# A chunked scan in which ScalarE makes one mask term before its other copies of a step, and VectorE adds the other mask term at the start of the next step

## The chip, the cores and the metric

The kernel runs on one core of one Trainium2 chip. The metric is the device time of one execution in microseconds (us), the median of three runs. Engines are named as in the profile: PE (TensorE matmul), PEld (its weight load), DVE (VectorE), ACT (ScalarE), POOL (GpSimd), SP (SyncE).

## The reference, cut to what matters

Two hybrid attention layers are followed by two layers whose token mixer is a bidirectional Mamba-2 scan beside windowed attention. The change lies in the scan, which runs once in each of the last two layers:

```
seg   = a_cum[..., :, None] - a_cum[..., None, :]
decay = exp(where(lower, seg, -inf))          # 128 x 128 for each head and chunk
mix   = (C @ B^T)[:, :, None] * decay
y     = mix @ (x * dt) + C @ prev * exp(a_cum)
```

The sequence of 512 is cut into 4 chunks of 128. There are 16 heads in 2 groups of 8. The reference does this for one direction; the kernel holds both directions in one 128 x 128 matrix for each head, the forward one below the diagonal and the backward one above it. So it needs, for each head, a matrix with dt of the forward direction on one triangle (mask "le") plus dt of the backward direction on the other (mask "ge"), which is then multiplied by C B^T and by exp of the summed decays.

## The kernel before, in words

Dense layers run as tiles of 128 x 128 weights by 512 tokens, three matmuls each (L523 to L525, high and low parts in fp32r), eight of them in a row into one PSUM bank `acc`. They fill TensorE's time between the pieces of the scan. The order of all work is written out by hand: each engine executes its own queue in program order.

A scan unit is one chunk and one group of 8 heads; there are 8 units in each scan. `run_units` walks through steps; in a step it emits, in this order and with two dense tiles (`fill`) behind each, piece `Vv` of the unit that began three steps ago, `Tt` of two steps ago, `S` of one step ago, and `S0` of the new unit. The first unit's `S0` is emitted earlier. Steps are numbered here by their `S`: step 1 holds the first `S`, and step 8 the last; "unit 1" is the unit whose `S` is in step 1.

- `S0`: POOL multiplies four tiles `adm` (L1772), one or two `xw` (L1688) and one `xd` (L1787): "the series" in what follows. ACT makes four `adm` tiles with 16 copies (L1778), then eight copies of mask "le" scaled by dt into two tiles `dm` (L1793), and DVE adds mask "ge" times dt to each (L1794, SCALAR_TENSOR_TENSOR on 128 x 128, both tensor inputs in SBUF).
- `S`: PE makes C B^T in bank `cb` (L1799) and the summed decays in two banks `gp` (L1806, from the `adm` tiles). DVE multiplies `dm` by `cb` (L1802, two instructions), ACT takes the exponential of `gp` in place (L1808), DVE multiplies `dm` by it (L1809, two instructions).
- `Tt`: PE applies earlier states (`yo`, L1817) and makes new ones (`stp`, L1744). DVE scales `yo` into `yoff` (L1819), POOL adds it to `xd` (L1820), DVE or ACT updates `state` (L1749 and L1750, or L1747).
- `Vv`: PE multiplies `dm` with the tokens into bank `yp` (L1829), DVE adds it to `xd` (L1831). Two steps later PE transposes `xd` into `ytp`, and DVE multiplies four tiles `z` by it (L1840).

The dense tiles bring their own work: DVE evacuates `acc` into `z` (L1708), ACT takes its tanh `zt` (L1710), DVE finishes `z` (L1711); ACT makes the weights' parts (L319, L324), and POOL issues an accumulating DMA on them (L320).

PSUM has eight banks, given out in turn: `bank()` takes the next one, whoever used it last. A bank's new owner on PE waits until the old owner's readers are done. Along the eight units this gives: the first `gp` of unit 2 lies where `cb` of unit 1 was, the last `stp` of step 4's `Tt` where `cb` of unit 3 was, `cb` of unit 5 where `cb` of unit 4 was, the first `gp` of unit 3 where `yp` of unit 1 was, and the second `gp` of unit 6 where the first `ytp` was.

Of the kernel before, what the change touches and what calls it, by code (L numbers as in the profile page):

```python
# [13 lines left out]
AF = mybir.ActivationFunctionType  # L14
OP = mybir.AluOpType
# [234 lines left out]
def trunk_kernel(ctx: ExitStack, tc: tile.TileContext, xT, positions, wts, cst_d, oh_d, rb_d, cw1_d,  # L250
# [4 lines left out]
    V, A, G, PE = nc.vector, nc.scalar, nc.gpsimd, nc.tensor  # L255
# [9 lines left out]
    def big(name, dt=F32):  # L265
        return pools["t"].tile([128, T], dt, tag="t", name=name)
# [7 lines left out]
    def bank(name, hold=False):  # L274
        b = banks.pop(0)
        t = psum.tile([128, T], F32, tag=f"b{b}", name=name)
        if hold:
            held[id(t)] = (b, t)
        else:
            banks.append(b)  # L280
        return t
# [121 lines left out]
    def C(name):  # L403
        o, n = _CS[name]
        return cst[:, o:o + n]
# [86 lines left out]
    def rstd_b(r4, name="R"):  # L492
        R = big(name)
        pb = spread(r4)
        V.tensor_copy(R, pb)
        free(pb)
        return R
# [1033 lines left out]
    def layer2(l, x, hs, sq, gnext):  # L1531
        P = prm[2, l]

        def pc(name):
            o, n = P2[name]
            return P[:, o:o + n]
# [54 lines left out]
        dt = {}  # L1591
# [87 lines left out]
        def bc64(ap):  # L1679
            return ap[:, :, None].to_broadcast([128, 8, 64])  # L1680

        def v8(ap):
            return ap.rearrange("p (h d) -> p h d", h=8)

        def weighted(c, g, d):
            assert all(4 * g + q in xdone for q in range(4))
            xw = big("xw")
            G.tensor_tensor(v8(xw), v8(xtok[c, g]), bc64(dt["w"][d][:, c, 8 * g:8 * g + 8]), OP.mult)  # L1688
            return xw
# [51 lines left out]
        def advance(prev, c, g, d, xw):  # L1741

            ps = bank("stp")
            PE.matmul(ps, btok[g][:, 128 * c:128 * c + 128], xw, start=True, stop=True)  # L1744
            new = big("state")
            if prev is None:
                A.activation(new, ps, AF.Copy)  # L1747
            else:
                V.tensor_tensor(v8(new), v8(prev), bc64(dt["cd"][:, c, d, 8 * g:8 * g + 8]), OP.mult)  # L1749
                V.tensor_add(new, new, ps)  # L1750
            return new
# [3 lines left out]
        def back_state(c, g, xw):  # L1755
            bwd[c - 1, g] = advance(bwd[c, g], c, g, 1, xw)
# [4 lines left out]
        def chunk_group(c, g):  # L1761
            u = {}
            t0 = 128 * c

            def S0():
                u["am"] = []
                for hb in range(2):
                    h0 = 8 * g + 4 * hb
                    am = []
                    for part in dt["adt"]:  # L1770
                        t = big("adm", F32R)
                        G.tensor_tensor(t.rearrange("p (h l) -> p h l", h=4),  # L1772
                                        C("le")[:, None, :].to_broadcast([128, 4, 128]),
                                        part[:, c, 0, h0:h0 + 4][:, :, None].to_broadcast([128, 4, 128]), OP.mult)
                        am.append((masks[0], t))
                        t = big("adm", F32R)
                        for hh in range(4):
                            A.activation(t[:, 128 * hh:128 * hh + 128], C("ge"), AF.Copy,  # L1778
                                         scale=part[:, c, 1, h0 + hh:h0 + hh + 1])
                        am.append((masks[1], t))  # L1780
                    u["am"].append(am)
                if c < 3:
                    u["xf"] = weighted(c, g, 0)
                if g == 0 and c:
                    u["xb"] = weighted(4 - c, 1, 1)
                xd = big("xd")
                G.tensor_tensor(v8(xd), v8(xtok[c, g]), bc64(pc("dsk")[:, 8 * g:8 * g + 8]), OP.mult)  # L1787
                u["xd"] = xd
                u["m"] = [big("dm") for _ in range(2)]
                for hh in range(8):  # L1790
                    h, sl = 8 * g + hh, slice(128 * (hh % 4), 128 * (hh % 4) + 128)
                    dm = u["m"][hh // 4]
                    A.activation(dm[:, sl], C("le"), AF.Copy, scale=dt["dt"][:, c, 0, h:h + 1])  # L1793
                    V.scalar_tensor_tensor(dm[:, sl], C("ge"), dt["dt"][:, c, 1, h:h + 1], dm[:, sl], op0=OP.mult,  # L1794
                                           op1=OP.add)

            def S():
                pcb = bank("cb")
                PE.matmul(pcb[:, 0:128], BT[g][:, t0:t0 + 128], CT[g][:, t0:t0 + 128], start=True, stop=True)  # L1799
                for dm in u["m"]:  # L1800
                    d4 = dm.rearrange("p (h l) -> p h l", h=4)
                    V.tensor_tensor(d4, d4, pcb[:, None, 0:128].to_broadcast([128, 4, 128]), OP.mult)  # L1802
                for dm, am in zip(u["m"], u.pop("am")):
                    gp = bank("gp")
                    for j, (mask, t) in enumerate(am):
                        PE.matmul(gp, mask, t, start=(j == 0), stop=(j == 3))  # L1806
                    e = gp
                    A.activation(e, gp, AF.Exp)  # L1808
                    V.tensor_mul(dm, dm, e)  # L1809

            def Tt():
                y = u["xd"]
                for d, prev in ((0, fwd[g]), (1, bwd[c, g])):
                    if prev is None:
                        continue
                    po = bank("yo")
                    PE.matmul(po, CT[g][:, t0:t0 + 128], prev, start=True, stop=True)  # L1817
                    t = big("yoff")
                    V.tensor_tensor(v8(t), v8(po), bc64(dt["e"][d][:, c, 8 * g:8 * g + 8]), OP.mult)  # L1819
                    G.tensor_add(y, y, t)  # L1820
                if "xb" in u:
                    back_state(4 - c, 1, u["xb"])
                if c < 3:
                    fwd[g] = advance(fwd[g], c, g, 0, u["xf"])

            def Vv():
                yp = bank("yp")
                for hh in range(8):
                    PE.matmul(yp[:, 64 * hh:64 * hh + 64], u["m"][hh // 4][:, 128 * (hh % 4):128 * (hh % 4) + 128],  # L1829
                              xtok[c, g][:, 64 * hh:64 * hh + 64], start=True, stop=True)  # L1830
                V.tensor_add(u["xd"], u["xd"], yp)  # L1831

                def back():
                    pt = bank("ytp")
                    for q in range(4):
                        PE.transpose(pt[:, 128 * q:128 * q + 128], u["xd"][:, 128 * q:128 * q + 128], ident)
                    yt[c, g] = pt
                    for q in range(4):
                        z = sz[4 * g + q]
                        V.tensor_mul(z[:, t0:t0 + 128], z[:, t0:t0 + 128], pt[:, 128 * q:128 * q + 128])  # L1840
                if c < 3:
                    return [(2, back)]

                def squares():
                    sg = st["sq", g] = Squares(4)
                    for q in range(4):
                        sg.add(sz[4 * g + q])

                def norm_a():
                    st["r4", g] = rstd_a(st.pop(("sq", g)), 512)  # L1850

                def norm_b():
                    st["Rg", g] = rstd_b(st.pop(("r4", g)), "Rg")

                def norm_c(q):
                    z = sz.pop(4 * g + q)
                    V.scalar_tensor_tensor(z, z, pc("sn")[:, 4 * g + q:4 * g + q + 1], st["Rg", g], op0=OP.mult,  # L1857
                                           op1=OP.mult)
                    h, lo = big("sh", F32R), big("sl", F32R)
                    split(h, lo, z, G)  # L1860
                    ysT[4 * g + q] = (h, lo)

                def norm_cs(at):
                    return [(at + q, lambda q=q: norm_c(q)) for q in range(4)]
                if g:
                    rest.extend([(1, back), (4, squares), (7, norm_a), (9, norm_b)] + norm_cs(10))
                    return []
                rest.extend(norm_cs(2))
                return [(2, back), (2, squares), (4, norm_a), (5, norm_b)]

            return (S0, S, Tt, Vv)

        ysT, rest = [None] * 8, []
# [61 lines left out]
        for a in range(8):  # L1935
# [20 lines left out]
            for e in range(2):  # L1956
                h = 2 * a + e
# [190 lines left out]
```

## Time and profile before

| | |
|---|---|
| median of 3 runs | 3185.03 us (3184.65 to 3185.07) |
| profiled execution, its own time | 3186.35 us |
| profiled execution, its span | 3184.6 us |
| PE busy | 3076.9 us, 97% of the span |
| DVE busy | 1986.2 us, 62% |
| ACT busy | 1663.1 us, 52% |
| POOL busy | 571.3 us, 18% |
| granted TensorE clock over the span | 0.985 |
| steps 1 to 8 of the first scan | 1704.14 to 1803.54 us of the span (first and last `cb`) |

Shares over the whole span mix stages. The two scans are about 100 us each, and there all engines are busy most of the time, so it is the order of waits in that stage that counts. The granted clock is the share of TensorE's full speed that the chip allowed in a stretch; 0.5 is its lower level.

### The profile page before, as it was taken

The numbers are of one execution on the slowest core, as the hardware profiler recorded it, in microseconds if no ns is written. First come the engines' busy times: TensorE is split into PE (matmuls) and PEld (weight loads), VectorE is DVE, ScalarE is ACT, GpSimd is POOL, SyncE is SP. The second block draws the span as 40 slices with busy tenths as digits, with TensorE's granted clock in tenths as the row PEclk, the third lists the DMA queues.
The fourth block names the chain that finished last, engine by engine and source line by source line (L and its number), as shares of the span: only waits on it lengthen the run. The fifth ranks groups of instructions, "written<-read, shape, count | busy, mean of one in ns | idle before, by whom it ended". The sixth has DMA issues, their size and how long they took to land. (4 is left out here: it accounts for less than half of the span.)

```text
span 3184.6 us, 41173 instructions
## 1 busy us (share of the span) xinstructions
PE 3076.9 (97%) x15086; PEld 2560.8 (80%) x15086; DVE 1986.2 (62%) x3707; ACT 1663.1 (52%) x3114; POOL 571.3 (18%) x558
## 2 busy tenths in 40 slices
PE   9999999999999999999999989999999998999998
PEld 8788888888778887888886768888888676888887
DVE  7677377374677737736576886463536688746353
ACT  4578544343357754434467677432346767744232
POOL 1222210001322221000225522000002553200000
PEclk9999999999899999999999999999999999999999
DMA  7743859575964384324585445634367543563331
GB/s 234 175 107 84 198 124 133 106 121 147 226 144 107 86 205 119 113 86 127 129 190 119 116 98 110 167 106 126 93 168 164 131 114 89 113 173 102 124 100 67
DMA packets 132806, 417.20 MB, mean 131 GB/s; under 512 B 15835, under 2 KB 20955, under 8 KB 132604
## 3 DMA queue, kind: packets, MB, share of 16 engines
q1 hardware_dynamic: 101500, 301.31, 31.8%
q0 software_dynamic: 31104, 113.26, 21.4%
q8 instruction: 119, 1.95, 0.3%
q14 instruction: 83, 0.68, 0.1%
HBM read 385.67 MB, written 20.97 MB: 128 GB/s over the span
## 5 line engine op out<-in xcount | busy, mean ns | idle before, releaser
L523 PE MATMUL acc<-h,wh 128*128 128x512 f32 (+1 forms) x2592 | 1019.5, 393 | 3.9 <-ACT h L419 3.9
L525 PE MATMUL acc<-hl,wh 128*128 128x512 f32 (+1 forms) x2592 | 993.6, 383 | 2.5 <-DVE hl L420 2.5
L524 PE MATMUL acc<-h,wl 128*128 128x512 f32 (+1 forms) x2592 | 993.4, 383 | 2.7 <-DVE wl L329 2.6
L525 PEld LDWEIGHTS acc<-hl,wh 128*128 128x128 f32 x2592 | 493.7, 190 | 98.7 <-DVE hl L420 4.2
L523 PEld LDWEIGHTS acc<-h,wh 128*128 128x128 f32 x2592 | 495.2, 191 | 93.9 <-issue 5.0
L524 PEld LDWEIGHTS acc<-h,wl 128*128 128x128 f32 x2592 | 495.3, 191 | 92.9 <-DVE wl L329 6.2
L320 POOL DMA_DIRECT2D wl<-in_wts x216 | 187.9, 870 | 1876.2 <-ACT wl L319 1321.1
L324 ACT ACTIVATE wh<-wraw 128x1024 fp32r<-128x1024 f32 x376 | 394.0, 1049 | 235.9 <-PE acc L525 200.3
L329 DVE TENSOR_TENSOR wl<-wraw,wh 128x1024 fp32r<-128x1024 f32 x244 | 297.2, 1220 | 90.6 <-ACT wh L324 82.9
L319 ACT ACTIVATE wl<-wraw 128x1024 fp32r<-128x1024 f32 x216 | 226.9, 1050 | 110.1 <-PE acc L524 105.5
L523 PE MATMUL acc<-ah,wh 128*128 128x512 f32 (+1 forms) x726 | 278.5, 384 | 0.0
L525 PE MATMUL acc<-al,wh 128*128 128x512 f32 (+1 forms) x726 | 278.1, 383 | 0.0
L524 PE MATMUL acc<-ah,wl 128*128 128x512 f32 (+1 forms) x726 | 278.1, 383 | 0.0
L1289 ACT ACTIVATE c<-u,prm 128x512 f32<-128x512 f32 x88 | 71.2, 815 | 189.3 <-DVE u L1285 189.3
L735 PE MATMUL pt<-cst,p 128*128 128x128 f32 x752 | 143.8, 279 | 24.8 <-ACT p L2075 9.8
L523 PEld LDWEIGHTS acc<-ah,wh 128*128 128x128 f32 x726 | 136.5, 188 | 26.7
L525 PEld LDWEIGHTS acc<-al,wh 128*128 128x128 f32 x726 | 136.5, 188 | 26.5
L524 PEld LDWEIGHTS acc<-ah,wl 128*128 128x128 f32 x726 | 136.5, 188 | 26.5
L741 ACT ACTIVATE pth<-pt 128x256 fp32r<-128x256 f32 (+2 forms) x320 | 130.7, 411 | 9.8 <-PE pt L735 7.5
L735 PEld LDWEIGHTS pt<-cst,p 128*128 128x128 f32 x752 | 93.3, 141 | 51.9 <-ACT p L2075 18.1
L1146 ACT ACTIVATE p<-p,nm 128x128 f32<-128x128 f32 x192 | 102.1, 532 | 61.8 <-DVE nm L1144 59.1
L1361 ACT ACTIVATE ah<-c 128x512 fp32r<-128x512 f32 x88 | 55.7, 633 | 137.7 <-DVE c L1358 137.5
(341 smaller groups left out, 5140.6 us busy)
## 6 DMA issues: line engine op xcount, KB each, us to landing
wraw<-in_wts SPq DMA_DIRECT2D x460, 512.0 KB, 5.0
wl<-in_wts POOLq DMA_DIRECT2D x216, 512.0 KB, 6.9
bias<-bias_d SPq DMA_DIRECT2D x32, 192.0 KB, 2.5
x<-in_xT SPq DMA_DIRECT2D x16, 256.0 KB, 7.3
cw<-in_cw SPq DMA_DIRECT2D x16, 256.0 KB, 6.1
xf<-x SPq DMA_DIRECT2D x16, 256.0 KB, 9.4
bias_d<-btab SPq DMA_DIRECT2D x16, 256.0 KB, 11.3
x<-xf SPq DMA_DIRECT2D x16, 256.0 KB, 5.6
```

The costliest lines, as they stand in the source:

```text
L319: A.activation(lo, r, AF.Copy, scale=-1.0)
L320: G.dma_start(out=lo, in_=wts[c], accum_op=OP.add)
L324: A.activation(h, r, AF.Copy)
L329: V.tensor_sub(lo, r, h.bitcast(F32))
L523: PE.matmul(acc, wh, xh, start=first, stop=False)
L524: PE.matmul(acc, wl, xh, start=False, stop=False)
L525: PE.matmul(acc, wh, xl, start=False, stop=last)
L735: PE.transpose(pt[:, 128 * n:128 * n + 128], t[:, 128 * (kb - b0):128 * (kb - b0) + 128], ident)
L741: A.activation(th[:, 0:w], pt[:, 0:w], AF.Copy)
L1146: A.activation(p[:, 0:w], p[:, 0:w], AF.Exp, bias=nm[:, col:col + 1], scale=-1.0, accum_out=den[:, col:col + 1])
L1289: A.activation(c, u, AF.Identity, bias=cb[:, idx:idx + 1], scale=cw[:, 88 + idx:89 + idx])
L1361: A.activation(h, a, AF.Copy)
```

## The change

The eight copies of ACT into `dm` move from the end of `S0` to its beginning, before the 16 copies into `adm`. The eight additions of DVE move from `S0` to `S` of the next step, before the two multiplications by `cb`. Every instruction stays, with the same operands; lines below the first edit move by one to six (the additions are L1799 now, the copies L1769).

```
             def S0():
                 u["am"] = []
+                u["m"] = [big("dm") for _ in range(2)]
+                for hh in range(8):
+                    A.activation(u["m"][hh // 4][:, 128 * (hh % 4):128 * (hh % 4) + 128], C("le"), AF.Copy,
+                                 scale=dt["dt"][:, c, 0, 8 * g + hh:8 * g + hh + 1])
                 for hb in range(2):
...
                 u["xd"] = xd
-                u["m"] = [big("dm") for _ in range(2)]
-                for hh in range(8):
-                    h, sl = 8 * g + hh, slice(128 * (hh % 4), 128 * (hh % 4) + 128)
-                    dm = u["m"][hh // 4]
-                    A.activation(dm[:, sl], C("le"), AF.Copy, scale=dt["dt"][:, c, 0, h:h + 1])
-                    V.scalar_tensor_tensor(dm[:, sl], C("ge"), dt["dt"][:, c, 1, h:h + 1], dm[:, sl], op0=OP.mult,
-                                           op1=OP.add)
 
             def S():
                 pcb = bank("cb")
                 PE.matmul(pcb[:, 0:128], BT[g][:, t0:t0 + 128], CT[g][:, t0:t0 + 128], start=True, stop=True)
+                for hh in range(8):
+                    dm, sl = u["m"][hh // 4], slice(128 * (hh % 4), 128 * (hh % 4) + 128)
+                    V.scalar_tensor_tensor(dm[:, sl], C("ge"), dt["dt"][:, c, 1, 8 * g + hh:8 * g + hh + 1],
+                                           dm[:, sl], op0=OP.mult, op1=OP.add)
                 for dm in u["m"]:
```

DVE's queue from `yoff` of step 2 to the multiplications of step 3, before:

```order
L1819 TENSOR_TENSOR yoff<-yo,ex 128x512
L1802 TENSOR_TENSOR dm<-dm,cb 128x512 x2
L1809 TENSOR_TENSOR dm<-dm,gp 128x512 x2
L1794 SCALAR_TENSOR_TENSOR dm<-cst,dt,dm 128x128 x8
L1831 TENSOR_TENSOR xd<-xd,yp 128x512
L1708 SCALAR_TENSOR_TENSOR z<-acc,R 128x512
L1711 SCALAR_TENSOR_TENSOR z<-zt,z 128x512
L1819 TENSOR_TENSOR yoff<-yo,ex 128x512 x2
L1749 TENSOR_TENSOR state<-state,ex 128x512
L1750 TENSOR_TENSOR state<-state,stp 128x512
L1802 TENSOR_TENSOR dm<-dm,cb 128x512 x2
L1809 TENSOR_TENSOR dm<-dm,gp 128x512 x2
```

The same place with the change:

```order
L1820 TENSOR_TENSOR yoff<-yo,ex 128x512
L1799 SCALAR_TENSOR_TENSOR dm<-cst,dt,dm 128x128 x8
L1803 TENSOR_TENSOR dm<-dm,cb 128x512 x2
L1810 TENSOR_TENSOR dm<-dm,gp 128x512 x2
L1832 TENSOR_TENSOR xd<-xd,yp 128x512
L1708 SCALAR_TENSOR_TENSOR z<-acc,R 128x512
L1711 SCALAR_TENSOR_TENSOR z<-zt,z 128x512
L1820 TENSOR_TENSOR yoff<-yo,ex 128x512 x2
L1749 TENSOR_TENSOR state<-state,ex 128x512
L1750 TENSOR_TENSOR state<-state,stp 128x512
L1799 SCALAR_TENSOR_TENSOR dm<-cst,dt,dm 128x128 x8
L1803 TENSOR_TENSOR dm<-dm,cb 128x512 x2
L1810 TENSOR_TENSOR dm<-dm,gp 128x512 x2
```

The additions no longer stand between the multiplications by `gp` and the addition of `yp`; they stand right before the multiplications by `cb`, behind `yoff` or the state.

ACT's queue from the exponentials of step 1 to the tanh of step 2, before:

```order
L1808 ACTIVATE gp<-gp 128x512 x2
L1778 ACTIVATE adm<-cst,adth 128x128 x4
L1778 ACTIVATE adm<-cst,adtl 128x128 x4
L1778 ACTIVATE adm<-cst,adth 128x128 x4
L1778 ACTIVATE adm<-cst,adtl 128x128 x4
L1793 ACTIVATE dm<-cst,dt 128x128 x8
L1710 ACTIVATE zt<-z 128x512
```

The same place with the change:

```order
L1809 ACTIVATE gp<-gp 128x512 x2
L1769 ACTIVATE dm<-cst,dt 128x128 x8
L1782 ACTIVATE adm<-cst,adth 128x128 x4
L1782 ACTIVATE adm<-cst,adtl 128x128 x4
L1782 ACTIVATE adm<-cst,adth 128x128 x4
L1782 ACTIVATE adm<-cst,adtl 128x128 x4
L1710 ACTIVATE zt<-z 128x512
```

The eight copies into `dm` now stand ahead of the 16 into `adm`. POOL's and PE's queues hold the same work in the same order as before.

## Rows read from the trace of the kernel before

**Rows 1.** The page, part 1: busy time, share, instructions by engine.

```profile
PE 3076.9 (97%) x15086; PEld 2560.8 (80%) x15086; DVE 1986.2 (62%) x3707; ACT 1663.1 (52%) x3114; POOL 571.3 (18%) x558
```

**Rows 2.** Waits of PE, first scan: us in total, times, longest.

```profile
PE gp L1806 <- DVE z L1840: 5.6, 1, 5.6
PE gp L1806 <- DVE xd L1831: 5.4, 1, 5.4
PE yo L1817 <- DVE state L1750: 1.3, 1, 1.3
PE gp L1806 <- ACT adm L1778: 0.9, 2, 0.4
```

**Rows 3.** The same view, second scan.

```profile
PE gp L1806 <- DVE xd L1831: 5.9, 2, 5.4
```

**Rows 4.** Stretches behind PE's two long waits; 1.00 would be the full clock.

```profile
1734.00:1739.40 5.40, 5.39 (x13) 4.25 (x14) 4.60 (x6) 4.90 (x10) 2.95 (x3) 0.50 0.25 30
1777.70:1783.80 6.10, 6.08 (x14) 4.78 (x15) 4.06 (x7) 4.00 (x13) 4.88 (x6) 0.50 0.62 130
```

**Rows 5.** Groups by line, first scan: busy, mean ns, idle before.

```profile
L1794 DVE SCALAR_TENSOR_TENSOR dm<-cst,dt,dm 128x128 f32<-128x128 f32 x64 | 28.2, 506 | 18.9 <-ACT dm L1793 18.9
```

**Rows 6.** Timeline, step 4: start us, us, engine, line.

```profile
1754.64 1.34 POOL L1772 TENSOR_TENSOR adm<-cst,adth 128x512 fp32r<-128x512 f32 x1
...
1755.35 1.28 DVE L1802 TENSOR_TENSOR dm<-dm,cb 128x512 f32<-128x512 f32 x2
...
1757.75 3.35 DVE L1794 SCALAR_TENSOR_TENSOR dm<-cst,dt,dm 128x128 f32<-128x128 f32 x1
...
1759.64 1.30 POOL L1787 TENSOR_TENSOR xd<-xtok,prm 128x512 f32<-128x512 f32 x1
```

**Rows 7.** Timeline early in the program: a run of DVE and POOL.

```profile
62.67 2.05 DVE L922 TENSOR_TENSOR gt<-t,prm 128x248 f32<-128x248 f32 x4
62.73 3.74 POOL L890 TENSOR_TENSOR swap<-swap,sinT 128x512 f32<-128x512 f32 x1 [1.60 <-DVE va L873]
64.65 0.67 DVE L889 TENSOR_TENSOR qaR<-qa,cosT 128x512 f32<-128x512 f32 x1
```

**Rows 8.** Timeline, step 1, in order of time.

```profile
1704.45 2.18 DVE L1794 SCALAR_TENSOR_TENSOR dm<-cst,dt,dm 128x128 f32<-128x128 f32 x8
...
1707.27 0.63 ACT L1710 ACTIVATE zt<-z 128x512 f32<-128x512 f32 x1 [0.87 <-DVE z L1708]
...
1709.71 1.37 POOL L1772 TENSOR_TENSOR adm<-cst,adth 128x512 fp32r<-128x512 f32 x1
...
1710.29 1.28 DVE L1802 TENSOR_TENSOR dm<-dm,cb 128x512 f32<-128x512 f32 x2
...
1715.71 1.33 POOL L1787 TENSOR_TENSOR xd<-xtok,prm 128x512 f32<-128x512 f32 x1
```

**Rows 9.** Timeline, step 3.

```profile
1739.83 1.28 DVE L1802 TENSOR_TENSOR dm<-dm,cb 128x512 f32<-128x512 f32 x2
1740.23 1.05 POOL L1772 TENSOR_TENSOR adm<-cst,adth 128x512 fp32r<-128x512 f32 x1
...
1745.29 1.08 POOL L1787 TENSOR_TENSOR xd<-xtok,prm 128x512 f32<-128x512 f32 x1
```

**Rows 10.** Timeline, step 5.

```profile
1766.27 1.67 POOL L1820 TENSOR_TENSOR xd<-xd,yoff 128x512 f32<-128x512 f32 x1 [5.33 <-DVE yoff L1819]
...
1767.50 1.28 DVE L1802 TENSOR_TENSOR dm<-dm,cb 128x512 f32<-128x512 f32 x2
1768.49 1.33 POOL L1772 TENSOR_TENSOR adm<-cst,adth 128x512 fp32r<-128x512 f32 x1
```

**Rows 11.** Timeline of PE, step 2.

```profile
1713.77 0.47 PE L1806 MATMUL gp<-adm,mask_gt 128*128 128x512 f32 x1
```

**Rows 12.** Timeline of PE, step 5, and of ACT, step 1 (a row of each).

```profile
1759.55 0.38 PE L1799 MATMUL cb<-c 128*128 128x128 f32 x2
...
1716.76 2.44 ACT L1793 ACTIVATE dm<-cst,dt 128x128 f32<-128x128 f32 x8
```

## The prediction, made before the changed kernel was run

> **What bounds the kernel now.** The page comes first: PE is busy 97% of the span [rows 1], so time can only be won where PE waits. The edit touches the two scans alone, so the waits of PE in those stretches come next. In the first scan PE waits 5.6 us for DVE's `z`, 5.4 us for DVE's `xd`, 1.3 us for `state` and 0.9 us for ACT's `adm` [rows 2]; that is 13.2 us. The second scan has the same pattern, its longest wait again 5.4 us [rows 3], so I work out one scan and double it. Both long waits are for PSUM banks: `gp` gets a bank whose reader on DVE is late. Behind each of them the granted clock is 0.50, for 5.4 and 6.1 us of PE work [rows 4], at the lower of the two levels (1.2 of 2.4 GHz), which costs half of that, 2.7 and 3.05 us. The room in one scan is therefore 13.2 + 5.75 = 18.95 us, in both 37.9 us, 1.2% of the time. No version of this edit can gain more.
>
> Why is DVE late? The groups by line show the additions of mask "ge" (L1794): DVE is idle 18.9 us ahead of them, waiting for ACT's copies, and the 64 additions take 506 ns on average [rows 5] while a run of eight in step 1 takes 2.18 us [rows 8], 0.26 us from one to the next. The second number is not slow arithmetic. In step 4 the first addition takes 3.35 us: it is issued at 1757.75, ends at 1761.10, and POOL's series ends at 1759.64 + 1.30 = 1760.94 [rows 6]. DVE was held until POOL's last instruction of the series was done. It goes the other way too: early in the program POOL's L890 is issued at 62.73, just behind a run of DVE instructions that ends at 65.32, and is done only at 66.47 [rows 7]; other instructions of POOL on such tiles take 1.3 to 1.4 us [rows 6, 8]. So an instruction of DVE that reads two SBUF tensors and one of POOL exclude each other, and whoever is first keeps the other out for its whole run. L1802 and L1809 read PSUM; in step 4 L1802 starts at 1755.35, inside the series, and its pair takes 1.28 us [rows 6], undisturbed.
>
> **What the edit removes.** DVE no longer waits for the copies (18.9 us in one scan), since a step passes between copy and addition. It evacuates `yp` and `ytp` several us earlier, so PE's waits of 5.4 and 5.6 us go, with the slow clock behind them: 5.4 + 5.6 + 2.7 + 3.05 = 16.75 us. In step 1 ACT waited 0.87 us for `z`, which stood behind the additions on DVE [rows 8]; without them `state` comes 0.9 us earlier and PE's wait of 1.3 us shrinks by that. The 0.9 us for `adm` falls under a longer wait (below). Together 18.55 us a scan.
>
> **What it adds.** The additions now stand where L1802 starts, and keep both multiplications behind them. What counts in each step is whether DVE comes there before POOL begins its series, for POOL's series holds the additions and L1802 did not mind it. The rows of before give both moments, and both follow from the same tanh or `yoff`, so their distance should last:
>
> - Step 1: series from 1709.71, L1802 at 1710.29 [rows 8]. POOL is first by 0.58 us.
> - Step 3: L1802 at 1739.83, series from 1740.23 [rows 9]; but POOL is still in the additions of `yoff` ahead of it, and the series follows without a gap. POOL again.
> - Step 4: 1754.64 against 1755.35 [rows 6]. POOL is first by 0.71 us.
> - Step 5: L1802 at 1767.50; POOL's addition of `yoff` ends at 1766.27 + 1.67 = 1767.94, the series starts at 1768.49 [rows 10]. The additions slip into that gap, and POOL waits for their 2.18 us. Steps 2, 6 and 7 stand in this order too, and step 8 has no series.
>
> Step 1, priced. The tanh starts at 1707.27 - 0.87 = 1706.40. The series ended 1715.71 + 1.33 - 1707.27 = 9.77 us after the tanh's start, so now at 1716.17. The eight additions end 0.16 + 7 x 0.26 = 1.98 us later, the pair on `cb` 1.28 us after that: 1719.43. PE's first `gp` of step 2 takes the bank of that `cb`. It started at 1713.77 [rows 11] and would be ready 0.87 us earlier, at 1712.90. **New wait 6.5 us**, plus 2.7 us of slow clock as behind the wait of 5.4 us: 9.2 us.
>
> Step 3: the additions are let go at the series' end, 1746.37, or 0.4 us behind it if POOL lets one through now and then; the pair on `cb` ends at 1748 instead of 1741.1 [rows 9]. The last `stp` of step 4 takes that bank. How far PE is by then I can only bound: 0, if PE is as late as DVE, to 5 us; I take 2, since PE comes out of step 2 some 6 us later than before and so has most of the 7 us behind it already.
>
> Step 4: DVE comes there about when it did (the extra 6 us of step 3 replace its waits for ACT and the hold that followed). The additions end at 1761.10 + 7 x 0.26 = 1762.92, the pair at 1764.20. PE's `cb` of step 5, at 1759.55 before [rows 12], needs the bank: **4.65 us**, plus 2.7 us of slow clock: 7.35 us.
>
> **What costs nothing, and its cover.** ACT makes `adm` 2.44 us later in each step, the time of the eight copies [rows 12]. This is covered where PE comes to `gp` later than that anyway: in step 2 by the 6.5 us wait, later by the dense tiles between. Without cover PE would wait up to 2.4 us in a step. Of the waits of POOL where DVE is first, 2.18 us each, `yoff` and `xd` have a whole step in reserve.
>
> **Sum.** Per scan 9.2 + 2 + 7.35 - 18.55 = 0.0 us, with 0 to 5 us for the one wait that I chose and about 2 us for each slow-clock term: -6 to +6 us, twice that for both scans. The profiled execution took 3186.35 us by itself (span 3184.6); the sum leaves it there, and the median of the runs is 1.3 us below it: **3185 us**. The wait that DVE had for ACT turns into a wait for POOL, and PE's two long stalls move to two other banks. Each of 0.2% is 6.4 us; a measurement of this kernel can tell about that from no change.
>
> **Rivals.**
>
> *DVE gets there first in step 1 as well.* Speaking for it: DVE loses by 0.58 us only. Against: the tanh from which both start is the same. The 9.2 us go, up to 2.4 us of `adm` come back: -6.8 us a scan, 3171 us. If step 4 went with it, -14 us a scan: 3157; with every new wait gone the bound is 3185 - 37 = 3148. Chance 0.24.
>
> *POOL lets DVE in after each of its instructions.* Then seven of the eight additions would pass during the series of step 1, 1.8 us earlier at its end, and as much in step 4: -3.6 us a scan, 3178 us. Against it stands the addition of 3.35 us, during which POOL began its next instruction, at 1759.64, without giving way [rows 6]. The Trainium skill, "SBUF — State Buffer", section "SBUF: two separate sides", says that the shared port pair is an exclusive lock and that whoever starts first holds it for the whole instruction. Read by the letter that would hand it over at the end of each instruction, as in this rival; the trace shows a hold over a run. Chance 0.11.
>
> *Slower: POOL is first in step 5 too.* There DVE is ahead by 0.99 us of the series, but arrives while POOL still adds `yoff`, and if POOL runs on into its series without the gap, the step is another step 4: its `cb` bank is missed by 7.35 us. One such step in each scan gives 3185 + 15 = 3200 us, and steps 5 to 7 all lost 3229. It decides from 0.5 us of delay on DVE, or from a POOL queue whose weight DMA, which makes the gap, comes earlier. Chance 0.22.
>
> **How the numbers follow.** The forecast of even sums has 0.43, with its own range 3174 to 3197: 0.09 of it falls below 3178.6, 0.26 within 0.2%, 0.08 above. The first rival is faster (0.24); the second splits 0.06 faster and 0.05 within; the third is slower (0.22). Faster 0.39, same 0.31, slower 0.30. Leaving out a tenth on either side, the ends lie within the first and the third rival: 3160 to 3205 us.
>
> **What would show it.** In the profile after, DVE's idle time ahead of the additions falls from 18.9 us to near nothing, but their mean duration rises well above 506 ns, with one addition of 6 us or more in steps 1 and 4. PE's waits for `xd` and `z` are gone; in their place `gp` of step 2 waits some 6.5 us, and `cb` of step 5 some 4 to 5 us, for DVE's multiplication by `cb` (L1803). If there is no wait at step 2, the first rival is at work; if additions of step 5 last 6 us, the third. I am wrong in kind if PE's new waits are for ACT's `adm` (L1782).

## The result, and the profile after

The changed kernel takes **3217.16 us** (median of 4 runs, 3214.48 to 3219.29), against 3185.05 us for the kernel before on the same chip: a ratio of 1.010, 95% interval 1.0085 to 1.0115. It is slower by 32 us; 3185 was predicted, in a range from 3160 to 3205.

The profiled execution's span is 3216.3 us, 31.7 more than before. Nearly all of it lies in the two scans: from the `cb` of step 1 to that of step 8 the first scan took 99.4 us before and takes 1819.34 - 1704.63 = 114.7 us now, 15.3 more, the second 114.6 in the place of 98.8, 15.8 more.

First the page: busy time of each engine and its share of the span (answers to [rows 1]).

```profile
PE 3083.1 (96%) x15086; PEld 2560.6 (80%) x15086; DVE 2056.4 (64%) x3707; ACT 1663.3 (52%) x3114; POOL 569.7 (18%) x558
```

DVE executes as many instructions as before and is busy for 70.2 us more. A DVE that is held by POOL counts as busy, so this is the first sign. The group of the additions, first scan (answers to [rows 5]: 28.2 us busy, 18.9 idle ahead of them):

```profile
L1799 DVE SCALAR_TENSOR_TENSOR dm<-cst,dt,dm 128x128 f32<-128x128 f32 x64 | 63.1, 1054 | 0.0
```

The wait for ACT is gone as predicted, and the additions take 34.9 us more; twice that is the 70 us of the page. Next, for whom PE waits in the first scan (answers to [rows 2]):

```profile
PE stp L1744 <- DVE dm L1803: 9.6, 4, 4.7
PE gp L1807 <- DVE dm L1803: 6.7, 1, 6.7
PE cb L1796 <- DVE dm L1803: 3.9, 1, 3.9
PE acc L523 <- DVE dm L1803: 3.6, 1, 3.6
PE yo L1818 <- DVE state L1750: 0.4, 1, 0.4
```

The waits for `z` and `xd` are gone, and 13.2 us of waiting have become 24.2, all but 0.4 of it for one instruction: DVE's multiplication by `cb` (L1803), which now stands behind the additions. The timeline of PE places each wait (idle time ahead of a row in brackets), between the first and the last `cb`:

```profile
1704.63 0.38 PE L1796 MATMUL cb<-c 128*128 128x128 f32 x2
...
1720.23 0.76 PE L1807 MATMUL gp<-adm,mask_gt 128*128 128x512 f32 x1 [6.71 <-DVE dm L1803]
...
1736.06 1.19 PE L1744 MATMUL stp<-xw,btok 128*128 128x512 f32 x1 [4.73 <-DVE dm L1803]
...
1752.16 0.67 PE L1744 MATMUL stp<-xw,btok 128*128 128x512 f32 x1 [0.83 <-DVE dm L1803]
...
1769.68 0.35 PE L1796 MATMUL cb<-c 128*128 128x128 f32 x1 [3.95 <-DVE dm L1803]
...
1785.66 0.76 PE L523 MATMUL acc<-h,wh 128*128 128x512 f32 x1 [3.64 <-DVE dm L1803]
...
1800.05 0.67 PE L1744 MATMUL stp<-xw,btok 128*128 128x512 f32 x1 [0.63 <-DVE dm L1803]
...
1815.42 1.19 PE L1744 MATMUL stp<-xw,btok 128*128 128x512 f32 x1 [3.44 <-DVE dm L1803]
...
1819.34 0.38 PE L1796 MATMUL cb<-c 128*128 128x128 f32 x2
```

Seven waits, one for the late multiplication of each of steps 1 to 7. The three that were predicted are the first (step 1), the third (step 3) and the fourth (step 4). Behind the long ones PE works at the lower clock, as in [rows 4] (windows: length, busy time and instructions of PE, PEld, DVE, ACT and POOL, granted clock, DMA share, GB/s):

```profile
1720.30:1723.20 2.90, 2.90 (x7) 2.32 (x8) 2.14 (x4) 1.23 (x2) 0.00 (x0) 0.50 0.00 0
1736.10:1740.10 4.00, 4.00 (x6) 1.84 (x7) 3.31 (x6) 1.76 (x3) 0.00 (x0) 0.50 0.02 4
1770.90:1774.00 3.10, 3.10 (x9) 2.42 (x8) 2.34 (x5) 1.98 (x3) 0.00 (x0) 0.51 0.02 5
1785.70:1791.20 5.50, 5.50 (x14) 4.44 (x15) 5.50 (x11) 0.62 (x2) 2.35 (x3) 0.50 0.34 95
1815.50:1818.60 3.10, 3.10 (x6) 1.78 (x7) 3.10 (x9) 0.00 (x0) 0.06 (x1) 0.50 0.00 0
```

18.6 us at 0.50 cost 9.3. Waits and clock make 24.2 + 9.3 = 33.5 us a scan, 14.6 more than the 18.95 of before: the measured difference but for about 1 us.

Last, DVE and POOL in step 2, where DVE was to be first (start, duration; the two rows at 1723.85 for L1799 are the first addition alone and the first two together):

```profile
1723.85 0.87 POOL L320 DMA_DIRECT2D wl<-in_wts  x1 [6.96 <-ACT wl L319]
1723.85 0.34 DVE L1799 SCALAR_TENSOR_TENSOR dm<-cst,dt,dm 128x128 f32<-128x128 f32 x1
1723.85 9.29 DVE L1799 SCALAR_TENSOR_TENSOR dm<-cst,dt,dm 128x128 f32<-128x128 f32 x2
1724.45 1.58 POOL L1821 TENSOR_TENSOR xd<-xd,yoff 128x512 f32<-128x512 f32 x1
1725.71 1.32 POOL L1776 TENSOR_TENSOR adm<-cst,adth 128x512 fp32r<-128x512 f32 x1
...
1731.70 1.28 POOL L1791 TENSOR_TENSOR xd<-xtok,prm 128x512 f32<-128x512 f32 x1
...
1734.63 1.28 DVE L1803 TENSOR_TENSOR dm<-dm,cb 128x512 f32<-128x512 f32 x2
```

One addition passes. The second is issued at 1724.11, 0.34 us ahead of POOL's first tensor operation in the trace (1724.45), and ends at 1723.85 + 9.29 = 1733.14, just behind the end of POOL's last product, 1732.98. DVE came first, and lost the rest of its run to POOL.

In step 5 DVE comes ahead of the series, but not ahead of POOL, which still adds `yoff`. The first addition ends with that one (0.59 us), and the second, issued 0.48 us before the series starts, is held to its end. Step 6 is the same (1.05 and 6.92 us).

```profile
1774.05 1.67 POOL L1821 TENSOR_TENSOR xd<-xd,yoff 128x512 f32<-128x512 f32 x1 [7.72 <-DVE yoff L1820]
1775.28 0.59 DVE L1799 SCALAR_TENSOR_TENSOR dm<-cst,dt,dm 128x128 f32<-128x128 f32 x1
1775.67 0.88 POOL L320 DMA_DIRECT2D wl<-in_wts  x1
1775.80 6.95 DVE L1799 SCALAR_TENSOR_TENSOR dm<-cst,dt,dm 128x128 f32<-128x128 f32 x1
1776.28 1.34 POOL L1776 TENSOR_TENSOR adm<-cst,adth 128x512 fp32r<-128x512 f32 x1
```

In step 7 not even one passes, though DVE's run begins 0.39 us ahead of the series:

```profile
1804.61 1.63 POOL L1821 TENSOR_TENSOR xd<-xd,yoff 128x512 f32<-128x512 f32 x1
1806.17 0.86 POOL L320 DMA_DIRECT2D wl<-in_wts  x1
1806.39 5.85 DVE L1799 SCALAR_TENSOR_TENSOR dm<-cst,dt,dm 128x128 f32<-128x128 f32 x1
1806.78 1.33 POOL L1776 TENSOR_TENSOR adm<-cst,adth 128x512 fp32r<-128x512 f32 x1
...
1810.78 1.30 POOL L1791 TENSOR_TENSOR xd<-xtok,prm 128x512 f32<-128x512 f32 x1
```

And in step 3 the two take turns, one for one; a run of 7.14 us all the same, since the series has six instructions:

```profile
1743.68 7.14 DVE L1799 SCALAR_TENSOR_TENSOR dm<-cst,dt,dm 128x128 f32<-128x128 f32 x8
1744.08 1.09 POOL L1776 TENSOR_TENSOR adm<-cst,adth 128x512 fp32r<-128x512 f32 x1
1745.13 1.08 POOL L1776 TENSOR_TENSOR adm<-cst,adtl 128x512 fp32r<-128x512 f32 x1
...
1749.32 1.08 POOL L1791 TENSOR_TENSOR xd<-xtok,prm 128x512 f32<-128x512 f32 x1
```

### The profile page after: what moved, and what is told of

Same layout as the page of the kernel before. It is cut to its first block, busy times and chain, and to the rows that moved or that the text cites. A ratio compares the mean times of both kernels' runs of the same rounds, so it can differ in the third digit from the quotient of the medians.

```text
span 3216.3 us, 41178 instructions
## 1 busy us (share of the span) xinstructions
PE 3083.1 (96%) x15086; PEld 2560.6 (80%) x15086; DVE 2056.4 (64%) x3707; ACT 1663.3 (52%) x3114; POOL 569.7 (18%) x558
## 5 line engine op out<-in xcount | busy, mean ns | idle before, releaser
L329 DVE TENSOR_TENSOR wl<-wraw,wh 128x1024 fp32r<-128x1024 f32 x244 | 297.1, 1220 | 89.7 <-ACT wh L324 82.1
```

The lines of the kernel that those rows point to most:

```text
L329: V.tensor_sub(lo, r, h.bitcast(F32))
```

## The experiments

**Theory**: the whole loss is POOL's hold on additions that read two SBUF tensors; whenever DVE comes, its run ends no earlier than POOL's series, and what stands behind the run is late by that. **Rivals**: ScalarE's new order (its `adm` comes later); the place of the additions on DVE by itself; some other limit of the scan. Twelve kernels tell them apart. "Scan" is the time from the first to the last `cb` of the first scan, "additions" their busy time there.

| kernel | median us | ratio to before, 95% interval | scan us | additions us |
|---|---|---|---|---|
| changed kernel | 3217.2 | 1.0100 (1.0085 to 1.0115) | 114.7 | 63.1 |
| copies alone | 3184.3 | 0.9995 (0.9986 to 1.0005) | 97.5 | 46.7 |
| additions alone | 3218.4 | 1.0105 (1.0088 to 1.0122) | 114.6 | 63.2 |
| changed, ge in PSUM | 3159.6 | 0.9920 (0.9906 to 0.9935) | 86.3 | 17.2 |
| additions ahead of yoff | 3167.7 | 0.9945 (0.9931 to 0.9960) | 88.4 | 34.0 |
| plain sums, 8 short | 3210.0 | 1.0078 (1.0058 to 1.0098) | 111.7 | 60.0 |
| plain sums, 2 long | 3197.7 | 1.0035 (1.0022 to 1.0049) | 104.0 | 51.4 |
| before, ge in PSUM | 3175.1 | 0.9967 (0.9954 to 0.9980) | 93.4 | 19.0 |
| copies alone, ge in PSUM | 3157.9 | 0.9913 (0.9896 to 0.9929) | 84.8 | 17.2 |
| ge in PSUM, copies last | 3155.1 | 0.9904 (0.9890 to 0.9919) | 82.1 | 17.2 |
| short series | 3167.1 | 0.9939 (0.9922 to 0.9955) | 87.9 | 36.4 |
| POOL waits for the last | 3158.0 | 0.9915 (0.9899 to 0.9932) | 85.8 | 21.7 |
| POOL waits for the second | 3190.1 | 1.0007 (0.9997 to 1.0017) | 98.5 | 47.9 |

**Which half does the harm? The copies alone** (this diff and those below are against the changed kernel, unless one says otherwise):

```diff
 def S0():
     ...
     u["xd"] = xd
+    for hh in range(8):
+        dm, sl = u["m"][hh // 4], slice(128 * (hh % 4), 128 * (hh % 4) + 128)
+        V.scalar_tensor_tensor(dm[:, sl], C("ge"), dt["dt"][:, c, 1, 8 * g + hh:8 * g + hh + 1],
+                               dm[:, sl], op0=OP.mult, op1=OP.add)
 def S():
     ...
-    for hh in range(8):
-        dm, sl = u["m"][hh // 4], slice(128 * (hh % 4), 128 * (hh % 4) + 128)
-        V.scalar_tensor_tensor(dm[:, sl], C("ge"), dt["dt"][:, c, 1, 8 * g + hh:8 * g + hh + 1],
-                               dm[:, sl], op0=OP.mult, op1=OP.add)
```

> Half of the change alone: ScalarE's copies go first in the step, VectorE's additions stay at the end of S0 as before. Theory (POOL's series of tensor operations is what holds the additions, before and after): in the trace of before the wait for the copies ended within about 2 us of the end of POOL's series (step 2: 1717.18 against 1717.04; step 3: the first addition came at 1729.27 and was held to 1731.4), so without the wait the additions come earlier and are held to the same moment: 3185 us, between 3180 and 3190, with additions of 3 to 6 us in the place of DVE's wait for ACT. Rival (the prediction's own step: DVE's 18.9 us of waiting for ACT were what made PE wait): PE's waits for xd and z go with their slow clock, 16 us a scan: 3150 to 3165. Second rival (ScalarE's adm, 2.4 us later in each step, costs): 3190 to 3205, with PE waiting for adm.

The time is that of before, as the theory had it. DVE's wait for ACT is 0.0 us in place of 18.9, and the additions take 46.7 us in place of 28.2: 18.5 us more. The wait went into the hold almost to the microsecond. PE waits 12.1 us in the first scan in place of 13.2: less for `z` and `xd` (4.8 and 2.8 us), more for ACT's `adm` (3.2 in place of 0.9). In the timeline the run of step 1 comes at 1714.45 (1717.18 before, in a step that began 1.5 us earlier), its first addition is held for 4.27 us, and it ends at 1720.56, 2 us behind the end of the series at 1718.56:

```profile
1714.45 6.11 DVE L1795 SCALAR_TENSOR_TENSOR dm<-cst,dt,dm 128x128 f32<-128x128 f32 x8
...
1717.23 1.33 POOL L1791 TENSOR_TENSOR xd<-xtok,prm 128x512 f32<-128x512 f32 x1
```

**The additions alone** (the additions in S as in the changed kernel; the copies left at the end of S0):

```diff
 def S0():
     u["am"] = []
-    u["m"] = [big("dm") for _ in range(2)]
-    for hh in range(8):
-        A.activation(u["m"][hh // 4][:, 128 * (hh % 4):128 * (hh % 4) + 128], C("le"), AF.Copy,
-                     scale=dt["dt"][:, c, 0, 8 * g + hh:8 * g + hh + 1])
     ...
     u["xd"] = xd
+    u["m"] = [big("dm") for _ in range(2)]
+    for hh in range(8):
+        A.activation(u["m"][hh // 4][:, 128 * (hh % 4):128 * (hh % 4) + 128], C("le"), AF.Copy,
+                     scale=dt["dt"][:, c, 0, 8 * g + hh:8 * g + hh + 1])
```

> The other half alone: VectorE's additions stand at the head of S as in the changed kernel, ScalarE's copies stay at the end of S0 as in the kernel before. Theory (the loss comes from additions that stand ahead of the multiplication by cb, where POOL's series holds them): as slow as the changed kernel, 3217 us (3209 to 3223), with a mean of the additions near 1054 ns. Rival (the copies ahead of adm on ScalarE share in the loss): clearly between the two kernels, 3190 to 3207.

As slow as the changed kernel, with the same waits of PE. The place of the additions does all of the harm that can be measured here, ScalarE's order none of it.

**The hold taken away, at the same place.** The additions read ge from PSUM:

```diff
     PE.matmul(pcb[:, 0:128], BT[g][:, t0:t0 + 128], CT[g][:, t0:t0 + 128], start=True, stop=True)
+    PE.transpose(pcb[:, 128:256], C("le"), ident)
     for hh in range(8):
         ...
-        V.scalar_tensor_tensor(dm[:, sl], C("ge"), ...
+        V.scalar_tensor_tensor(dm[:, sl], pcb[:, 128:256], ...
```

> The changed kernel, with the mask ge of the additions read from PSUM: TensorE transposes le (whose transpose is ge) into the free columns of the bank of cb, one 128x128 transpose a step, 16 in all, and the additions stay where they are. Theory (POOL excludes only an instruction of DVE that reads two SBUF tensors): a run of eight takes 2.2 to 2.5 us in every step although POOL's series runs beside it, the mean of the additions falls from 1054 to about 300 to 350 ns a piece busy, PE's waits for cb multiplications go, and the time comes near the room that the trace of before showed, 3148 plus some 5 us for the transposes: 3155 us (3148 to 3170). Rival (POOL's work holds any instruction of DVE, or the loss comes from the place of the additions on DVE alone, not from POOL): additions still held, 3205 to 3220.

Held nowhere: 343 ns an addition, 2.15 us a run in every step, and 57.5 us less than the changed kernel, with the same instructions on DVE and POOL at the same places. Step 1, beside a series that started before the run:

```profile
1711.02 1.37 POOL L1776 TENSOR_TENSOR adm<-cst,adth 128x512 fp32r<-128x512 f32 x1
...
1711.24 2.15 DVE L1800 SCALAR_TENSOR_TENSOR dm<-cb,dt,dm 128x128 f32<-128x128 f32 x8
...
1714.02 1.34 POOL L1776 TENSOR_TENSOR adm<-cst,adtl 128x512 fp32r<-128x512 f32 x1
```

This decides between the theory and the rivals: only the operand's memory differs (and 16 transposes more on PE).

**A third place for the additions**, ahead of the next step's `yoff`, for which POOL waits (in step 1, which has no Tt, they stay in S; the function that is put on the list holds the loop that S loses):

```diff
 def S0():
     ...
+    todo.append(add)
 def S():
     ...
-    for hh in range(8):
-        dm, sl = u["m"][hh // 4], slice(128 * (hh % 4), 128 * (hh % 4) + 128)
...
+    while todo:
+        todo.pop()()
 def Tt():
+    while todo:
+        todo.pop()()
     y = u["xd"]
```

> The changed kernel with the additions at a third place: ahead of the next step's evacuation of yo into yoff, where POOL waits for yoff and has no series under way. Theory: each run of eight takes 2.2 us, without a hold; both multiplications run beside POOL's series: 3155 us (3148 to 3168). Rival (yoff comes 2.2 us later, so POOL's series and its adm do too, and the loss turns up at gp on PE): 3175 to 3195 us, with PE waiting for POOL's adm or for yo. Second rival (the place of the additions does not matter): 3210 to 3220.

Slower than S with PSUM, but 50 us faster than the changed kernel. Three runs take 2.2 us and one 3.0, but in four (9.10 us in step 1, and 3.9 to 6.0 in three later ones) a series was still under way. Where DVE meets no series it is not held; the place has to miss the series in every step, and this one does so in half of them.

**The series cut short.** POOL's four products left out:

```diff
     for part in dt["adt"]:
-        t = big("adm", F32R)
-        G.tensor_tensor(t..., C("le")..., part[:, c, 0, ...]..., OP.mult)
-        am.append((masks[0], t))
         t = big("adm", F32R)
         for hh in range(4):
             A.activation(t[:, 128 * hh:128 * hh + 128], C("ge"), AF.Copy, ...
-        am.append((masks[1], t))
+        am += [(masks[0], t), (masks[1], t)]
```

> The changed kernel with POOL's four products for adm left out (TensorE reads ScalarE's adm for both masks, so that the result is not that of the reference): POOL's series shrinks by 4 us in each step, nothing of DVE or of the additions' operands changes. Theory (a run of additions lasts until POOL's series ends): the runs of steps 1 and 4 to 7 fall by 4 us each, that of step 1 from 9.1 to about 5, the busy time of the additions in the first scan from 63 to 35 us or less, and the time falls most of the way to the kernel before or below it: 3170 us (3158 to 3190). Rival (something else than the length of POOL's series sets the hold): runs as long as before, 3208 to 3220.

Every run that meets a series shrinks with it: step 1 from 9.10 to 5.13 us, steps 2 and 4 to 7 by 3.7 to 4.0 each (10.87 to 6.91, 7.60 to 3.62, and so on), and step 3, where they take turns, from 7.14 to 3.99. The hold has the length of the series.

**Who is let in? The form of DVE's instructions.** Two kernels with plain sums, first eight short ones:

```diff
-        V.scalar_tensor_tensor(dm[:, sl], C("ge"), dt[...], dm[:, sl], op0=OP.mult, op1=OP.add)
+        V.tensor_tensor(dm[:, sl], C("ge"), dm[:, sl], OP.add)
```

and, in the place of that loop, for the long ones

```diff
+    for dm in u["m"]:
+        d4 = dm.rearrange("p (h l) -> p h l", h=4)
+        V.tensor_tensor(d4, C("ge")[:, None, :].to_broadcast([128, 4, 128]), d4, OP.add)
```

> The changed kernel with its eight additions of a step as plain sums of two SBUF tensors (tensor_tensor, 128x128 each), without the weight dt, which is left out of the result: it asks why DVE's runs keep POOL out in the rows of the early program (L922/L889, tensor_tensor) and not in the scan. Theory (the form decides: a run of tensor_tensor leaves POOL no opening, a run with a scalar operand does): in steps 2, 5 and 6, where DVE is first, the run takes 2 to 2.5 us in the place of 9 to 11, POOL's next instruction 2 us or more in the place of 1.3, and the time falls to 3190 to 3207. Rival (POOL gets in behind whichever instruction of DVE is running when it asks, whatever its form): runs of 9 to 11 us in steps 2, 5 and 6 and 3217 us (3208 to 3222).

> The same with two sums of 128x512 a step in the place of eight of 128x128 (the weight dt left out of the result as well): it asks whether the number of openings between DVE's instructions matters. Theory (POOL gets in behind the instruction that runs when it asks): with two instructions of 0.6 us each, the second is still held to the end of POOL's series in steps 2, 5 and 6 unless POOL asks later than 0.6 us behind the first; runs of 1.2 us where POOL comes later, 7 to 9 us where it comes earlier; 3190 to 3217 us, nearer the upper end. Rival (the run is kept whole): 1.2 us in all three steps, 3185 to 3203.

The form doesn't matter. In step 2 the short kernel's third sum is held for 8.90 us (below: the first two sums, then the second and third together), the long one's second for 9.11. POOL gets in between the instructions of either run.

```profile
1721.69 0.87 POOL L320 DMA_DIRECT2D wl<-in_wts  x1 [6.53 <-ACT wl L319]
1721.70 0.48 DVE L1799 TENSOR_TENSOR dm<-cst,dm 128x128 f32<-128x128 f32 x2
1721.89 9.11 DVE L1799 TENSOR_TENSOR dm<-cst,dm 128x128 f32<-128x128 f32 x2
1722.30 1.59 POOL L1820 TENSOR_TENSOR xd<-xd,yoff 128x512 f32<-128x512 f32 x1
```

The long kernel's time was forecast nearer 3217 than it came out: with two sums a step, step 3's run takes 2.44 us where eight took 7.14 by turns. That run ends at 1744.58, 4.9 us before POOL's series does: where they take turns, two sums need only two of its openings.

**The order forced, both ways.** POOL copies one column of an addition's result ahead of its series, so that it comes behind that addition, in one kernel the last of the eight:

```diff
         V.scalar_tensor_tensor(dm[:, sl], C("ge"), ...
+    G.tensor_copy(small(1, "turn", bufs=2), u["m"][1][:, 511:512])
     for dm in u["m"]:
```

> The changed kernel with the turn given to DVE: ahead of its series POOL copies one column (128x1) of what the last of the eight additions wrote, so that the series begins behind the run in every step, and POOL gives up 2 to 3 us of the 5 to 7.7 us in which it is idle in a step. Operands, places and the result stay. Theory (the loss is the hold by the series and nothing else): runs of 2.2 us, up to 3.3 where POOL's addition of yoff is still under way; both multiplications beside the series; PE's waits for the multiplication by cb gone: 3157 us (3150 to 3168). Rival (a later series is itself a loss, since PE then waits for POOL's adm): 3170 to 3190, with PE waiting for L1776.

59 us faster than the changed kernel, with every operand where it was. The runs take 2.2 us in four steps, 2.4 in steps 3 and 5, where POOL's addition of `yoff` overlaps them, and 3.9 and 4.2 in steps 2 and 6. PE waits 2.3 us in the first scan for ACT's `adm`, never for POOL's: the later series costs nothing. This run also shows that POOL's DMA issue alone does not hold DVE. In step 5 three additions are issued during it, at least 1.46 us before POOL's next operation, and take 0.34 us each (the 2.43 us are the whole run of eight):

```profile
1755.85 2.43 DVE L1799 SCALAR_TENSOR_TENSOR dm<-cst,dt,dm 128x128 f32<-128x128 f32 x8
1756.24 0.88 POOL L320 DMA_DIRECT2D wl<-in_wts  x1
```

In the other kernel it is the second:

```diff
         V.scalar_tensor_tensor(dm[:, sl], C("ge"), ...
+        if hh == 1:
+            G.tensor_copy(small(1, "turn", bufs=2), dm[:, 255:256])
     for dm in u["m"]:
```

> The same with the column that the second of the eight additions wrote: POOL comes out of a wait into the middle of DVE's run in each step, as its L890 did in the rows of the early program. Theory (POOL gets in whenever it asks, behind the addition that is running): additions 4 to 8 wait for the end of the series, runs of 8 to 10 us in all seven steps, 3217 us (3208 to 3225). Rival (the rule of the prediction, good for a POOL that comes out of a wait: it is kept out until DVE's run ends, and the breaks in steps 2, 5 and 6 came from POOL being at work already): runs of 2.2 to 3 us, POOL's small copy or first product 2 us long, 3157 us (3150 to 3170). Second rival (they take turns one by one, as in step 3): runs of 6 to 7 us, 3200 to 3212.

Between the forecasts; the second rival's mechanism, in five of seven steps. Four additions are issued ahead of the series (the third and fourth while POOL's copy is on its way) and the rest take turns with the series, so the runs are 5.3 to 7.1 us, shorter than was worked out for six by turns. These runs end ahead of the series (step 1: 1713.82 against 1716.72), which the theory did not allow. In steps 5 and 6 the fifth is held for 6.3 us to the series' end. POOL is kept out in none. Step 1:

```profile
1708.50 1.13 DVE L1799 SCALAR_TENSOR_TENSOR dm<-cst,dt,dm 128x128 f32<-128x128 f32 x4
1709.17 0.24 POOL L1802 COPY turn<-dm 128x1 f32<-128x1 f32 x1 [0.60 <-DVE dm L1799]
1709.29 4.53 DVE L1799 SCALAR_TENSOR_TENSOR dm<-cst,dt,dm 128x128 f32<-128x128 f32 x5
1709.38 1.15 POOL L1776 TENSOR_TENSOR adm<-cst,adth 128x512 fp32r<-128x512 f32 x1
```

**Where the expected gain had gone.** The additions stay at their old place, and the wait for ACT (the run of the copies alone, above) and the hold are taken away one by one and together. For the hold, against the kernel before and against that run:

```diff
 def S0():
+    ge = gex[0]
     ...
-        V.scalar_tensor_tensor(dm[:, sl], C("ge"), ...
+        V.scalar_tensor_tensor(dm[:, sl], ge, ...
 def S():
     ...
+    PE.transpose(pcb[:, 128:256], C("le"), ident)
+    gex[0] = pcb[:, 128:256]
```

> The kernel before with only the hold taken away: its additions at the end of S0 read ge from the bank of the last cb, into which TensorE transposes le (seven of the eight steps of a scan; unit 0 reads SBUF, its run was not held). The copies of ScalarE stay where they were. Theory (in the kernel before the wait for the copies and the hold by POOL's series end at about the same moment, so either alone covers for the other): additions of 0.34 us each, DVE's wait for ACT unchanged or longer, and little gain: 3180 us (3172 to 3188). Rival (the hold alone cost the time of before): 3150 to 3165.

> The copies first (as in the run of the copies alone, 3184 us) and the hold taken away as well, with the additions left at the end of S0. Theory (both had to go): additions of 0.34 us each with no wait for ACT, PE's waits for xd and z gone, near the 3160 us of the changed kernel with ge in PSUM: 3158 us (3150 to 3168). Rival (the place of the additions, ahead of cb's multiplication or behind gp's, matters by itself, or the bank of cb, kept some 3 us longer, makes PE wait): 3172 to 3187.

Without the wait: nothing that can be told from 0; without the hold: 10 us; without both: 27 us. The 10 us are no clean price of the hold. In that run DVE still waits 20.8 us for ACT, PE no longer waits for `z` or `xd`, and 7.9 us of its waits in the first scan are for the additions (L1796), which now read the bank of `cb` and keep it while they wait for ACT. The kernel before has no such wait. The longest:

```profile
PE gp L1810 <- DVE dm L1796: 5.6, 1, 5.6
```

How much of the 17 us from 10 to 27 is the wait for ACT by itself, and how much that bank, no run separates. Once both are gone the additions' place hardly matters (3157.9 at the end of S0, 3159.6 in S).

**The fastest version**: additions in S, ge in PSUM, the copies last as in the run of the additions alone.

> The fastest version so far (additions in S, ge in PSUM, 3160 us) with ScalarE's copies back at the end of S0. Theory (the 2.6 us a scan for which PE still waits for ACT's adm come from the copies ahead of it): these waits go, twice 2.6 us: 3154 us (3149 to 3158), and the additions do not wait for the copies, which have a step in reserve. Rival (the wait is covered by the next one, or the additions then wait for ACT): 3158 to 3170.

3155.1 us, 30 less than before. PE's wait for `adm` falls from 2.6 us in the version with the copies first to the row below, about what the forecast had. The room read from the trace of before ended at 3148.

```profile
PE gp L1808 <- ACT adm L1778: 0.9, 2, 0.4
```

## Why the prediction was wrong

**The step that failed** is, in its words, "whoever is first keeps the other out for its whole run", and what it made of steps 2, 5, 6 and 7: "The additions slip into that gap, and POOL waits for their 2.18 us". POOL's series does keep DVE out, in every step but 3, where they take turns. A run of DVE does not keep POOL out: in step 2 DVE was first, one addition passed, and the second waited 9.03 us. The kernels with plain sums and the one in which POOL waits for the second addition showed the same with other forms and lengths and with POOL coming out of a wait. The rule was drawn from one place ([rows 7]). Why DVE's run did keep POOL out there stays open; no run here repeats it.

The gap was none. In steps 5 and 6 DVE came while POOL was adding `yoff`: one addition got in behind that, and the next waited 6.9 us. In step 7 none passed. The held additions were issued 0.34 to 0.48 us before POOL's next tensor operation starts in the trace, during its DMA issue. The DMA issue alone holds nothing (POOL waits for the last, above); why they were held before the operation's recorded start stays open. In step 2 there was no gap to begin with: POOL's addition of `yoff` runs on into its series (1724.45 + 1.58 = 1726.03, against 1725.71).

For steps 5 to 7 that is the third rival's mechanism, "POOL runs on into its series without the gap". Its figure with all three lost, 3229, came nearest to the result, in part by luck: it has 22 us for them where 12.0 were measured in the first scan, and nothing for step 2, which cost 6.7. The rows from which it could have been given more than 0.22 stood there: [rows 10] show POOL's addition ending at 1767.94, behind the arrival of DVE at 1767.50.

**By its terms** (first scan, each wait with half of the slow stretch behind it):

- Removed: 18.55 us predicted. Right: no wait for `z`, `xd` or ACT's copies is left, and 0.4 us of `state` remains.
- Step 1: 9.2 predicted, 6.71 + 1.45 = 8.2 measured; the wait itself was 6.5 against 6.71. Right.
- Step 3: 2 predicted (0 to 5), 0.8 measured. Right.
- Step 4: 7.35 predicted, 3.95 + 1.55 = 5.5 measured. Right in place, too large.
- Steps 2, 5, 6 and 7: 0 predicted; 4.73 + 2.0, 3.64 + 2.75, 0.63, and 3.44 + 1.55 measured: 18.7 us together. This is the error, more than the whole loss of a scan.
- ACT's `adm`, later by 2.44 us: nothing predicted, nothing measured in the changed kernel, where PE does not wait for it. With the other waits gone it shows, at 2.6 us a scan.

**The rivals.** "DVE gets there first in step 1 as well": POOL was first, and the first addition took 7.26 us. "POOL lets DVE in after each of its instructions": so it does in step 3 and, when POOL waits for the second addition, in five steps. In step 3 this saves nothing: seven of the eight additions come one to an instruction of POOL, and the run lasts 7.14 us. In all other steps of the changed kernel that meet a series it does not. The Trainium skill, "SBUF — State Buffer", section "SBUF: two separate sides", has the shared pair held for a whole instruction against a VectorE instruction with two SBUF inputs. That the operands decide is what the run with ge in PSUM shows (343 ns an addition against 1054). For the length of a hold the measurement decides: 9.03 us (1724.11 to 1733.14), across eight tensor operations of POOL.

One premise of the sum fell as well. The prediction counted DVE's 18.9 us wait for ACT as the cause of PE's waits; the run of the copies alone shows that taking it away by itself gives nothing, since POOL's series then holds the additions to about the same moment. In the run with the hold alone taken away PE does not wait for `z` or `xd` although DVE still waits for ACT; but PE is held up earlier there, so this does not settle what the wait for ACT is worth.

## What to carry to other kernels

Before moving a VectorE instruction that reads two SBUF tensors, look at what GpSimd does at its new place: here a run of them was mostly held to the end of GpSimd's series, whoever started first, or went on at one instruction of VectorE for each of GpSimd's, and what matters is what stands behind the run (here the multiplication that frees a bank of PE). Ways out, each worth 57 to 59 us here against the changed kernel: read one operand from PSUM, or make GpSimd wait for the run if it has the time. When two causes end a wait at about the same moment, taking one away can show nothing, as the copies alone did; take away both before judging either, and see whether the test itself adds a wait.

## What was unexpected of the hardware

A series of POOL shows in two forms. Where its rows overlap (1.3 us long, 1.00 us apart) DVE's addition is held to the end of the series; where they hardly do (1.08 us long, 1.05 apart) DVE gets one addition in after each. Step 2 and step 3 above show one each; steps 3 and 4 of before ([rows 9], [rows 6]) show the same pair, in which it was overlooked: 1.05 us a row in step 3, 1.3 in step 4. The form is there before DVE asks: in step 3 of before the series starts at 1740.23 and the additions come at 1743.51. What puts POOL into one form or the other was not tried. Where its next instruction has to wait (the copy of one column) the form with hardly any overlap followed in most steps.
